# Making the first weight sum of a seven-product pair by two GpSimd transfers, and taking 43 pairs instead of 32 that way

## The chip, the cores and the metric

The kernel runs on one core of one Trainium2 chip. The metric is the device time of one execution in microseconds. The engines are named as the profile names them: PE is TensorE (PEld its weight loads), DVE is VectorE, ACT is ScalarE, POOL is GpSimd, and SP is SyncE, which here only issues transfers.

## The reference

An encoder trunk of two layers, width 2048, 256 tokens, 256 memory tokens, feed-forward width 8192, all in float32. Each layer has an attention sub-layer (12 heads, and 4 heads into the memory), an output projection, and a squared-ReLU feed-forward part. The change lies in that last part alone:

```python
for i in range(DEPTH):
    ...
    x = x + heads @ w_out[i]
    h = rms_norm(x, norm_mlp[i])
    x = x + jnp.square(jax.nn.relu(h @ w_up[i])) @ w_down[i]
```

`w_up[i]` is 2048 x 8192 and `w_down[i]` is 8192 x 2048.

## The kernel before, in words

Every float32 product is made of three matmuls: each operand is split into a high part (a rounded copy, by ACT) and a low part (the rest, by DVE), and PE adds high x high, high x low and low x high (`split` and `three`). PE works through the weights in pieces of 128 x 1024 (512 KB). SP loads a piece into `raw`, ACT casts it to `hi`, DVE subtracts to `lo`; each of the three has four buffers. `piece` hands a piece to PE and keeps two more in preparation (`AHEAD = 2`).

The down projection is done in two halves of 1024 output columns per layer (`half_`, or `h` in the plan). One half goes over 64 pieces, two at a time: pair `j` (0 to 31) covers 256 rows of the hidden and has two blocks of hidden rows, two blocks of tokens and two blocks of 512 columns, that is eight block products of three matmuls, 24 in all. The products of a half collect in four PSUM banks, `ps`.

For the pairs in `FAST` the eight block products are done as seven, by Strassen's scheme in Winograd's form (`seven`): 21 matmuls. They need sums of weight blocks and of hidden blocks, and four more PSUM banks, `side`, which `add_side` combines once after the last such pair. The sums of weights are made when the second piece of the pair is fetched (`fetch_sums`): `a` (two blocks side by side) is the first piece plus the upper half of the second piece, which is added to both; `b` is made from `a`, the first piece and the second piece, in two steps. `a` and `b` are then split like any other weights into `ah`, `al`, `bh`, `bl`.

These six tiles (128 x 1024 each) come from a pool of eight buffers called `x2`. In the second half of layer 0 four of the eight hold the next layer's input, so there `a` and `b` are taken from `blk`, ten buffers that hold the hidden and come free as it is used up. The middle part of the hidden lies in one large tile, `big`, which takes the relative-position bias of layer 1 as soon as it is free: SP copies it back, and POOL masks it with two selects (`bias_load`).

Engines work in order. The order is made when the program is built, by a scheduler that moves instructions among each other where their data allow; so the code's order is not the engines' order, and a look at it is given below.

Of the kernel before, what the change touches and what calls it, by code (L numbers as in the profile page):

```python
# [19 lines left out]
ALU = mybir.AluOpType  # L20
AX = mybir.AxisListType

P = 128
# [9 lines left out]
WAIT = 2  # L33
AHEAD = 2
WARM = 16
FAST = (5, 8, 11, 14, 17, 20, 23, 26)
LAM_INIT = 0.8 - 0.6 * math.exp(-0.3 * 0)

G_ATTN, G_MEM, G_MLP = 0, 2 * KT, 4 * KT
# [8 lines left out]
def trunk(ctx: ExitStack, tc: tile.TileContext, xin, xtok, memin, pos, rel, gcol, rows,  # L48
          w_a, w_b, w_mem, w_out, w_up, w_down, out):
    nc = tc.nc  # L50
# [10 lines left out]
    def nm(s):  # L61
        uid[0] += 1
        return f"{s}{uid[0]}"

    def bank(tag="aux"):
        return pp.tile([P, 512], F32, tag=tag, name=nm(tag))

    def quad(tag, shape=(P, 2, 2, 256), dt=F32R):
        return xp.tile(list(shape), dt, tag=tag, name=nm(tag), bufs={"x2": 8, "h2": 6, "blk": 10}[tag])
# [92 lines left out]
    def flush():  # L162
        while tasks:
# [3 lines left out]
    weights = {"a": w_a, "b": w_b, "mem0": w_mem[0], "mem1": w_mem[1], "out0": w_out[0], "out1": w_out[1],  # L167
               "up0": w_up[0], "up1": w_up[1], "down0": w_down[0], "down1": w_down[1]}
    plan = deque()

    def plan_chunks(name, chunks):
        plan.extend((name, c, j) for c in chunks for j in range(8))

    def plan_down(name):
        plan.extend((name, h, j) for h in range(2) for j in range(64))

# [12 lines left out]
    def fetch_sums(key, raw, hi, lo):  # L189

        first = newest[0]
        tag = "blk" if key[:2] == ("down0", 1) else "x2"
        a, b = quad(tag, (P, 2, 512), F32), quad(tag, (P, 2, 512), F32)
        nc.vector.tensor_tensor(a, first.rearrange("p (a n) -> p a n", a=2),
                                raw[:, 512:1024].unsqueeze(1).broadcast_to([P, 2, 512]), op=ALU.add)
        nc.vector.tensor_tensor(b[:, 0, :], a[:, 1, :], first[:, 0:512], op=ALU.add)
        nc.vector.tensor_tensor(b[:, 1, :], b[:, 0, :], raw[:, 0:512], op=ALU.add)
        split(hi[:, 0:512], lo[:, 0:512], raw[:, 0:512])
        ah, al, bh, bl = [quad("x2", (P, 2, 512)) for _ in range(4)]
        split(ah, al, a)  # L200
        split(bh, bl, b)
        sums[key] = (ah, al, bh, bl)

    def fetch(parts=1, lead=None):

        name, c, j = plan.popleft()
        src = weights[name][c, j]
        raw = wp.tile([P, 1024], F32, tag="raw", name=nm("raw"))
        hi = wp.tile([P, 1024], F32R, tag="hi", name=nm("hi"))
        lo = wp.tile([P, 1024], F32R, tag="lo", name=nm("lo"))  # L210
        n = 1024 // parts
        seven = name.startswith("down") and j % 2 == 1 and j // 2 in FAST
        for i in range(parts):
            s = slice(i * n, (i + 1) * n)
            if lead is not None:
                lead(i)
            behind[0] = nc.sync.dma_start(raw[:, s], src[:, s])
            if seven:
                fetch_sums((name, c, j), raw, hi, lo)
            else:  # L220
                split(hi[:, s], lo[:, s], raw[:, s])
        newest[0] = raw
        ready.append(((name, c, j), hi, lo))
# [16 lines left out]
    def split(hi, lo, src):  # L240
        nc.scalar.copy(hi, src)  # L241
        nc.vector.tensor_tensor(lo, src, as32(hi), op=ALU.subtract)  # L242
# [437 lines left out]
    def mlp(layer, X2, last):  # L680
# [24 lines left out]
        for half_ in range(2):  # L705
            tag = "mm" if half_ == 0 else "aux"
            ps = [[bank(tag) for _ in range(2)] for _ in range(2)]
            chunks = (2 * half_, 2 * half_ + 1)

            def three(bank_, first_, last_, x2, xs, w2, ws):  # L710
                nc.tensor.matmul(bank_, lhsT=x2[:, 0, xs], rhs=w2[0][:, ws], start=first_, stop=False)  # L711
                nc.tensor.matmul(bank_, lhsT=x2[:, 0, xs], rhs=w2[1][:, ws], start=False, stop=False)  # L712
                nc.tensor.matmul(bank_, lhsT=x2[:, 1, xs], rhs=w2[0][:, ws], start=False, stop=last_)  # L713

            lower, upper = slice(0, 512), slice(512, 1024)

            def mms(n, t, k, two, x2):
                w2 = two[(k + n) % 2]
                three(ps[n][t], k == 0, k == 4 * KT - 1, x2, slice((k % 2) * S + t * P, (k % 2) * S + (t + 1) * P), w2,
                      upper if n else lower)  # L720

            def seven(j, two, x2):

                ah, al, bh, bl = [v.rearrange("p a n -> p (a n)") for v in sums.pop((f"down{layer}", half_, 2 * j + 1))]
                t2 = quad("h2", (P, 2, 512))
                v = t2k([P, 512])
                h = hidden(j)
                h4 = h.rearrange("p (a s) -> p a s", a=4)
                nc.vector.tensor_tensor(v[:, 0:256].rearrange("p (a s) -> p a s", a=2), h4[:, 0:4:3, :],
                                        h4[:, 1:2, :].broadcast_to([P, 2, P]), op=ALU.subtract)  # L730
                nc.vector.tensor_tensor(v[:, 256:384], h[:, 384:512], v[:, 0:128], op=ALU.add)
                nc.vector.tensor_tensor(v[:, 384:512], h[:, 256:384], v[:, 256:384], op=ALU.subtract)
                split(t2[:, 0, :], t2[:, 1, :], v)
                at = [slice(i * P, (i + 1) * P) for i in range(4)]
                f, e = j == FAST[0], j == FAST[-1]
                three(side[0], f, e, x2, at[0], two[0], lower)
                three(ps[0][0], False, False, x2, at[2], two[1], lower)
                three(ps[1][0], False, False, t2, at[3], two[0], upper)
                three(side[1], f, e, t2, at[0], (ah, al), upper)
                three(side[3], f, e, t2, at[1], (ah, al), lower)  # L740
                three(side[2], f, e, t2, at[2], (bh, bl), lower)
                three(ps[0][1], False, False, x2, at[3], (bh, bl), upper)

            def add_to(n, t, src):
                c = chunks[n]
                d = xt[:, t, c * 512:(c + 1) * 512]
                nc.vector.scalar_tensor_tensor(d, src, r2[:, t:t + 1], d, op0=ALU.mult, op1=ALU.add)
                return c, d

            def add_side():  # L750

                q1, u2, u3, u4, u5 = [t2k([P, 512]) for _ in range(5)]
                nc.scalar.copy(q1, side[0])
                nc.vector.tensor_tensor(u2, side[2], q1, op=ALU.subtract)
                nc.vector.tensor_tensor(u4, side[1], u2, op=ALU.subtract)
                nc.vector.tensor_tensor(u3, u2, side[3], op=ALU.subtract)
                nc.vector.tensor_tensor(u5, u3, side[1], op=ALU.subtract)
                add_to(0, 0, q1)
                add_to(0, 1, u4)
                add_to(1, 0, u3)  # L760
                add_to(1, 1, u5)

            def finish(n, t):
                c, d = add_to(n, t, ps[n][t])
                if last:
                    nc.sync.dma_start(out[:, t * D + c * 512:t * D + (c + 1) * 512], d)

            held = []
            for j in range(32):
                if j == FAST[0]:  # L770
                    side = [bank("aux" if half_ == 0 else "mm") for _ in range(4)]
                two = [piece(f"down{layer}", half_, 2 * j + i) for i in range(2)]
                x2 = h2_of(j)
                if last and half_ == 1 and j >= 30:
                    held.append((j, two, x2))
                    continue
                if j in FAST:
                    seven(j, two, x2)
                else:
                    for kk in range(2):  # L780
                        for t in range(2):
                            for n in range(2):
                                mms(n, t, 2 * j + kk, two, x2)
                if j == FAST[-1]:
                    add_side()
                tick()
                tick()
            for n in range(2):
                for t in range(2):
                    for j, two, x2 in held:  # L790
                        for kk in range(2):
                            mms(n, t, 2 * j + kk, two, x2)
                    finish(n, t)
                if not last:
                    chunk_sq(chunks[n])
                    to_features(chunks[n], N2, G_ATTN + KT, tag)
# [73 lines left out]
    for g in range(3):  # L870
        ps = chunk_tok("b", g, X2)
        qT, qd = norm_T(ps, st1, 4, gs[:, 1:2])
        for h in range(4):
            n = 4 * g + h
# [71 lines left out]
```

## Time and profile before

| | |
|---|---|
| time, median of 3 runs | 2127.89 us (2127.4 to 2128.0) |
| the profiled execution | 2127.94 us, of which its span 2126.1 us |
| granted clock of TensorE | 0.999 |
| PE, DVE, ACT, POOL busy | 2116.4, 1497.5, 1130.8, 34.3 us |
| HBM read, mean rate | 401.93 MB, 192 GB/s |
| weight load of 512 KB for the down projection, from issue to landing | 4.3 us, median of 256 |

The down projection of layer 0 runs from about 785 to 1125 us of the span, that of layer 1 from about 1784 us to the end. PE is busy all the time, so the rows are to be read for two things: how many matmuls there are, and how far ahead of PE the other engines are when they deliver. A row of a group gives line, engine, operation, output and inputs, shapes and count, then busy time and mean duration, then the idle time before them and who ended it. A row of the timeline gives start, duration, and how many instructions were merged.

### The profile page before, as it was taken

The numbers are of one execution on the slowest core, as the hardware profiler recorded it, in microseconds if no ns is written. First come the engines' busy times: TensorE is split into PE (matmuls) and PEld (weight loads), VectorE is DVE, ScalarE is ACT, GpSimd is POOL, SyncE is SP. The second block draws the span as 40 slices with busy tenths as digits, with TensorE's granted clock in tenths as the row PEclk, the third lists the DMA queues.
The fourth block names the chain that finished last, engine by engine and source line by source line (L and its number), as shares of the span: only waits on it lengthen the run. The fifth ranks groups of instructions, "written<-read, shape, count | busy, mean of one in ns | idle before, by whom it ended". The sixth has DMA issues, their size and how long they took to land.

```text
span 2126.1 us, 29324 instructions
## 1 busy us (share of the span) xinstructions
PE 2116.4 (100%) x11020; PEld 1790.6 (84%) x11020; DVE 1497.5 (70%) x2259; ACT 1130.8 (53%) x1712; POOL 34.3 (2%) x61
## 2 busy tenths in 40 slices
PE   9999999999999999999999999999999999999999
PEld 7878878888888888888888888888888888888887
DVE  7667786566565558889886677655555556888896
ACT  6456675454444446656655566554444444665564
POOL 1200020000000000000000000000000000000000
PEclk9999999999999999999999999999999999999999
DMA  8864564666666655555766556466666666566654
GB/s 292 238 211 150 159 194 154 186 180 190 191 184 196 188 190 200 197 198 198 250 205 191 178 167 187 149 180 188 188 189 190 186 192 193 190 215 210 203 193 158
DMA packets 114958, 409.23 MB, mean 192 GB/s; under 512 B 13568, under 2 KB 14336, under 8 KB 114560
## 3 DMA queue, kind: packets, MB, share of 16 engines
q1 hardware_dynamic: 111840, 401.01, 59.7%
q0 software_dynamic: 1536, 4.20, 0.8%
q10 hardware_dynamic: 1440, 2.15, 0.3%
q8 instruction: 86, 1.41, 0.3%
q14 instruction: 56, 0.46, 0.1%
HBM read 401.93 MB, written 5.37 MB: 192 GB/s over the span
## 4 chain that ended last, share of the span: by engine, by line
PE 97%; DMA 1%; DVE 1%; ACT 1%; issue 0%; SPq 0%; POOL 0%; ACTq 0%; DVEq 0%; POOLq 0%
PE mm L325 11%; PE aux L325 11%; PE mm L312 9%; PE mm L314 9%; PE mm L313 9%; PE mm L329 6%; PE aux L329 6%; PE aux L711 5%; PE aux L712 5%; PE mm L711 5%; PE mm L712 5%; PE aux L713 5%; PE mm L713 5%; PE aux L404 1%; DMA raw<-in_w_a 1%; PE aux L375 1%
## 5 line engine op out<-in xcount | busy, mean ns | idle before, releaser
L242 DVE TENSOR_TENSOR lo<-raw,hi 128x1024 fp32r<-128x1024 f32 (+1 forms) x744 | 875.4, 1190 | 535.3 <-ACT hi L241 534.0
L241 ACT CAST hi<-raw 128x1024 fp32r<-128x1024 f32 (+1 forms) x744 | 751.7, 1024 | 760.9 <-PE aux L325 193.5
L312 PE MATMUL mm<-hi,x 128*128 128x512 f32 x704 | 281.5, 401 | 0.7 <-ACT hi L241 0.7
L313 PE MATMUL mm<-lo,x 128*128 128x512 f32 x704 | 276.8, 393 | 2.6 <-DVE lo L242 2.6
L314 PE MATMUL mm<-hi,x 128*128 128x512 f32 x704 | 276.5, 393 | 0.0
L325 PE MATMUL mm<-x,hi 128*128 128x512 f32 x1024 | 247.4, 391 | 0.0
L325 PE MATMUL aux<-x,hi 128*128 128x512 f32 x1024 | 246.9, 391 | 0.0
L325 PEld LDWEIGHTS mm<-x,hi 128*128 128x128 f32 x1024 | 188.2, 188 | 36.8 <-DVE xt L675 0.5
L325 PEld LDWEIGHTS aux<-x,hi 128*128 128x128 f32 x1024 | 188.2, 188 | 36.4
L712 PE MATMUL aux<-lo,h 128*128 128x512 f32 x432 | 168.2, 389 | 0.0
L713 PE MATMUL aux<-hi,h 128*128 128x512 f32 x432 | 168.1, 389 | 0.0
L711 PE MATMUL aux<-hi,h 128*128 128x512 f32 x432 | 168.1, 389 | 0.0
L711 PE MATMUL mm<-hi,h 128*128 128x512 f32 x432 | 168.0, 389 | 0.0
L712 PE MATMUL mm<-lo,h 128*128 128x512 f32 x432 | 168.0, 389 | 0.0
L713 PE MATMUL mm<-hi,h 128*128 128x512 f32 x432 | 168.0, 389 | 0.0
L313 PEld LDWEIGHTS mm<-lo,x 128*128 128x128 f32 x704 | 133.1, 189 | 28.4 <-DVE lo L242 4.2
L314 PEld LDWEIGHTS mm<-hi,x 128*128 128x128 f32 x704 | 132.6, 188 | 28.0
L312 PEld LDWEIGHTS mm<-hi,x 128*128 128x128 f32 x704 | 132.6, 189 | 27.2 <-ACT hi L241 1.3
L329 PEld LDWEIGHTS mm<-x,lo 128*128 128x128 f32 x1024 | 131.4, 191 | 4.8
L329 PEld LDWEIGHTS aux<-x,lo 128*128 128x128 f32 x1024 | 131.3, 191 | 5.0
L329 PE MATMUL mm<-x,lo 128*128 128x256 f32 x1024 | 133.3, 283 | 0.0
L329 PE MATMUL aux<-x,lo 128*128 128x256 f32 x1024 | 132.8, 283 | 0.0
(207 smaller groups left out, 2526.0 us busy)
## 6 DMA issues: line engine op xcount, KB each, us to landing
raw<-in_w_up SPq DMA_DIRECT2D x256, 512.0 KB, 3.8
raw<-in_w_down SPq DMA_DIRECT2D x256, 512.0 KB, 4.3
raw<-in_w_a SPq DMA_DIRECT2D x72, 512.0 KB, 4.0
raw<-in_w_out SPq DMA_DIRECT2D x64, 512.0 KB, 3.6
raw<-in_w_b SPq DMA_DIRECT2D x48, 512.0 KB, 3.7
raw<-in_w_mem SPq DMA_DIRECT2D x32, 512.0 KB, 4.0
raw<-in_w_a SPq DMA_DIRECT2D x16, 256.0 KB, 5.2
blk<-bkt POOLq DMA_DIRECT2D x32, 128.0 KB, 8.6
```

The source lines that it names most:

```text
L241: nc.scalar.copy(hi, src)
L242: nc.vector.tensor_tensor(lo, src, as32(hi), op=ALU.subtract)
L312: nc.tensor.matmul(ps[t], lhsT=xh, rhs=hi[:, ws], start=(k == 0), stop=False)
L313: nc.tensor.matmul(ps[t], lhsT=xh, rhs=lo[:, ws], start=False, stop=False)
L314: nc.tensor.matmul(ps[t], lhsT=xl, rhs=hi[:, ws], start=False, stop=(k == KT - 1))
L325: nc.tensor.matmul(ps[o], lhsT=hi[:, cols(k % 2, o)], rhs=x2.rearrange("p a s -> p (a s)"), start=(k == 0), stop=(k == 2 * nj - 1))
L329: nc.tensor.matmul(ps[o][:, 256:512], lhsT=lo[:, cols(k % 2, o)], rhs=x2[:, 0, :], start=False, stop=False)
L375: nc.tensor.transpose(out=pt[:, h * P:(h + 1) * P], in_=qn[t][:, h * P:(h + 1) * P], identity=ident)
L404: nc.tensor.transpose(out=pt[:, kt * S + qt * P:kt * S + (qt + 1) * P], in_=p_of(qt)[:, kt * P:(kt + 1) * P], identity=ident)
L711: nc.tensor.matmul(bank_, lhsT=x2[:, 0, xs], rhs=w2[0][:, ws], start=first_, stop=False)
L712: nc.tensor.matmul(bank_, lhsT=x2[:, 0, xs], rhs=w2[1][:, ws], start=False, stop=False)
L713: nc.tensor.matmul(bank_, lhsT=x2[:, 1, xs], rhs=w2[0][:, ws], start=False, stop=last_)
```

## The change

Three things. `a` is no longer added by DVE from `raw`: POOL's queue loads the first piece a second time from HBM straight into `a`, and then issues a second transfer that reads the upper half of the second piece, twice, and adds it to what lies in `a`. The list of pairs is denser: 11 pairs in the halves that use `FAST`, two in every five, instead of 8, one in three. And the second half of layer 0 has a list of its own, `LATE`, with 10 pairs. Together that is 3 x 11 + 10 = 43 pairs instead of 4 x 8 = 32.

```diff
-FAST = (5, 8, 11, 14, 17, 20, 23, 26)
+FAST = (3, 5, 8, 10, 13, 15, 18, 20, 23, 25, 28)
+LATE = (6, 8, 11, 13, 16, 18, 21, 23, 26, 28)
...
+    def fast_pairs(name, h):
+        return LATE if (name, h) == ("down0", 1) else FAST
...
         a, b = quad(tag, (P, 2, 512), F32), quad(tag, (P, 2, 512), F32)
-        nc.vector.tensor_tensor(a, first.rearrange("p (a n) -> p a n", a=2),
-                                raw[:, 512:1024].unsqueeze(1).broadcast_to([P, 2, 512]), op=ALU.add)
+        src = weights[key[0]][key[1]]
+        nc.gpsimd.dma_start(a, src[key[2] - 1].rearrange("p (a n) -> p a n", a=2))
+        nc.gpsimd.dma_start(a, src[key[2]][:, 512:1024].unsqueeze(1).broadcast_to([P, 2, 512]), accum_op=ALU.add)
         nc.vector.tensor_tensor(b[:, 0, :], a[:, 1, :], first[:, 0:512], op=ALU.add)
         nc.vector.tensor_tensor(b[:, 1, :], b[:, 0, :], raw[:, 0:512], op=ALU.add)
...
-        seven = name.startswith("down") and j % 2 == 1 and j // 2 in FAST
+        seven = name.startswith("down") and j % 2 == 1 and j // 2 in fast_pairs(name, c)
...
+            fast = fast_pairs(f"down{layer}", half_)
...
-                f, e = j == FAST[0], j == FAST[-1]
+                f, e = j == fast[0], j == fast[-1]
...
-                if j in FAST:
+                if j in fast:
                     seven(j, two, x2)
...
-                if j == FAST[-1]:
+                if j == fast[-1]:
                     add_side()
```

The change adds six lines ahead of most of the code. So after it the two transfers are L199 and L200, the two steps of `b` are L201 and L202 (L196 and L197 before; the sum of `a` was L194), the split is L246 and L247 (L241 and L242), and the selects are L621 and L623 (L616 and L618).

How DVE is ordered around pair 23 in the first half of layer 0, before: `x21674` is `a`, `x21675` is `b`, `x21677` and `x21679` are the low parts of the two, `raw1668` and `raw1671` the two pieces of the pair, `h...` splits of the hidden for other pairs.

```order
L242 TENSOR_TENSOR h21709_8902<-blk1354_7167,h21709_8902 128x512
L194 TENSOR_TENSOR x21674_8753<-raw1668_8743,raw1671_8749 128x1024
L196 TENSOR_TENSOR x21675_8754<-x21674_8753,raw1668_8743 128x512
L197 TENSOR_TENSOR x21675_8754<-x21675_8754,raw1671_8749 128x512
L242 TENSOR_TENSOR x21677_8761<-x21674_8753,x21676_8760 128x1024
L242 TENSOR_TENSOR x21679_8763<-x21675_8754,x21678_8762 128x1024
L242 TENSOR_TENSOR lo1670_8745<-raw1668_8743,hi1669_8744 128x1024
L242 TENSOR_TENSOR lo1673_8751<-raw1671_8749,hi1672_8750 128x512
```

The same place after: `x21690` is `a` (now written by the transfers), `x21691` is `b`, `x21693` and `x21695` are their low parts, `raw1684` and `raw1687` the two pieces, and the first two rows are the pieces of pair 22.

```order
L247 TENSOR_TENSOR lo1679_8748<-raw1677_8746,hi1678_8747 128x1024
L247 TENSOR_TENSOR lo1682_8754<-raw1680_8752,hi1681_8753 128x1024
L201 TENSOR_TENSOR x21691_8796<-x21690_8795,raw1684_8785 128x512
L247 TENSOR_TENSOR h21718_8907<-blk1354_7167,h21718_8907 128x512
L202 TENSOR_TENSOR x21691_8796<-x21691_8796,raw1687_8791 128x512
L247 TENSOR_TENSOR x21693_8804<-x21690_8795,x21692_8803 128x1024
L247 TENSOR_TENSOR h21725_8946<-blk1354_7167,h21725_8946 128x512
L247 TENSOR_TENSOR x21695_8806<-x21691_8796,x21694_8805 128x1024
L247 TENSOR_TENSOR lo1686_8787<-raw1684_8785,hi1685_8786 128x1024
```

The row of the first sum is gone, and two splits of the hidden now stand between the steps; the first row that needs the transfers is L201, and `lo1686`, which PE needs first in the pair, stands behind it.

On POOL, which before had nothing between the norm of the memory and the two selects, the transfers of the second half of layer 0 stand before and behind the selects. After (`blk1997` is `a` of pair 21, `blk2019` of pair 23, `blk2048` of pair 26):

```order
L199 DMA blk1997_10201<-in_w_down 128x1024
L200 DMA blk1997_10201<-in_w_down 128x2x512
L621 AFFINE_SELECT big2116_10758<-big2116_10758 128x12x128
L623 AFFINE_SELECT big2116_10758<-big2116_10758 128x12x128
L199 DMA blk2019_10297<-in_w_down 128x1024
L200 DMA blk2019_10297<-in_w_down 128x2x512
L199 DMA blk2048_10432<-in_w_down 128x1024
```

Before, in the same place:

```order
L254 TENSOR_TENSOR acc_100<-acc_100,t1k692_3459 128x256
L254 TENSOR_TENSOR acc_100<-acc_100,t1k693_3462 128x256
L616 AFFINE_SELECT big2076_10652<-big2076_10652 128x12x128
L618 AFFINE_SELECT big2076_10652<-big2076_10652 128x12x128
L941 UNCONDITIONAL_BRANCH
```

The transfers of pair 23 and of all later pairs of this half have moved behind the selects, which themselves wait for SP's copy into `big`.

More of the change, by code (lines that the diff above doesn't have):

```diff
@@ L769, in mlp @@
             for j in range(32):
-                if j == FAST[0]:
+                if j == fast[0]:
                     side = [bank("aux" if half_ == 0 else "mm") for _ in range(4)]
```

## The prediction

> **What bounds the kernel now.** I read the page first, then the busy time by stretch, then single rows of TensorE and VectorE inside a seven-product pair.
>
> ```profile
> span 2126.1 us, 29324 instructions
> PE   2116.4 (100%) x11020; PEld 1790.6 (84%) x11020; DVE 1497.5 (70%) x2259; ACT 1130.8 (53%) x1712; POOL 34.3 (2%) x61
> PE 97%; DMA 1%; DVE 1%; ACT 1%; issue 0%; SPq 0%; POOL 0%; ACTq 0%; DVEq 0%; POOLq 0%
> L712 PE MATMUL aux<-lo,h 128*128 128x512 f32 x432 | 168.2, 389 | 0.0
> L712 PE MATMUL mm<-lo,h 128*128 128x512 f32 x432 | 168.0, 389 | 0.0
> ```
>
> PE (TensorE) carries 97% of the chain that ended last, and the matmuls of the down projection never stand behind an idle PE (0.0 in the last column). So a matmul that is left out there is worth its full pitch, and anything that makes PE wait there is paid in full. The pitch is read from the starts, since the 389 ns of one matmul overlap the next. These are the first and the last row of seven-product pair 11 in the first half of layer 0, and the first row of pair 12:
>
> ```profile
> 843.81 0.39 PE L711 MATMUL aux<-hi,h 128*128 128x512 f32 x1
> 844.04 0.39 PE L712 MATMUL aux<-lo,h 128*128 128x512 f32 x1
> ...
> 848.35 0.39 PE L713 MATMUL mm<-x,h 128*128 128x512 f32 x1
> 848.57 0.39 PE L711 MATMUL mm<-hi,h 128*128 128x512 f32 x1
> ```
>
> 21 matmuls take 848.57 - 843.81 = 4.76 us, 0.2267 us each; an ordinary pair has 24 and takes 5.44 us. What runs beside it is seen in two stretches (PE, PEld, DVE, ACT, POOL busy, granted clock, share of the DMA engines, GB/s):
>
> ```profile
> 811.00:961.00 150.00, 150.00 (x668) 124.32 (x667) 130.16 (x153) 91.71 (x118) 0.00 (x0) 1.00 0.59 202
> 1811.00:1961.00 150.00, 150.00 (x663) 124.21 (x662) 132.21 (x164) 89.69 (x110) 0.00 (x0) 1.00 0.62 209
> ```
>
> DVE (VectorE) is 87% busy there, ACT 61%, POOL (GpSimd) not at all, and the clock is whole. DVE is the next engine in line.
>
> **What the change takes off PE.** 11 pairs more go by seven products: 11 x 3 = 33 matmuls fewer, 33 x 0.2267 = 7.48 us. The profiled execution took 2127.94 us (its span is 2126.1; the median of the runs is 2127.89), so with no new wait it would take 2120.5 us. Nothing in the change can bring more than that, since PE has no idle time in these stages to give back.
>
> **What it does to DVE and ACT.**
>
> ```profile
> L242 DVE TENSOR_TENSOR x<-x,x 128x1024 fp32r<-128x1024 f32 x48 | 58.3, 1221 | 0.0
> L242 DVE TENSOR_TENSOR lo<-raw,hi 128x512 fp32r<-128x512 f32 x48 | 32.9, 686 | 0.2
> L194 DVE TENSOR_TENSOR x<-raw,raw 128x1024 f32<-128x1024 f32 x24 | 29.4, 1224 | 11.4 <-DMA raw<-in_w_down 11.4
> L242 DVE TENSOR_TENSOR h<-t2k,h 128x512 fp32r<-128x512 f32 x32 | 21.9, 684 | 0.0
> L197 DVE TENSOR_TENSOR x<-x,raw 128x512 f32<-128x512 f32 x24 | 16.6, 691 | 0.7
> L241 ACT CAST x<-x 128x1024 fp32r<-128x1024 f32 x48 | 50.6, 1053 | 82.1 <-DVE x L194 74.9 <-DVE x L197 7.2
> ```
>
> The first sum leaves DVE: 32 x 1.22 = 39 us less. Each further seven costs DVE two sums of 0.69, two low parts of 1.22, one low part of 0.68, three small differences (0.42 for the first, its row stands in the next group; the two others are half its size, so about 1.0 together is an estimate), and saves 0.54 on the half piece: about 5.0 us, 11 times, 55 us. So DVE does 16 us more over four halves, 4 us each. In 150 us it stands idle for 20, so I cost this at nothing; if that cover were gone, the 4 us a half would show as waits of PE for `lo`. ACT gains two casts of 1.05 for each further seven, beside 39% idle: nothing.
>
> **What it puts on the path: two transfers in a row.** `a` is now loaded by POOL's queue, POOL waits for the landing, then issues the accumulating transfer, and DVE's L201 waits for that. Behind L201 on DVE, which works in order, stand the splits that PE needs next. So the question is how long the two take (call it D) and how long they may take.
>
> How long they may: a seven uses six of the eight x2 buffers, so where FAST holds in the x2 pool the load of `a` can start only when PE is through with the seven before the last. For pair 23 that is pair 18. From the end of 18 to the start of 23 PE has pairs 19, 21, 22 (24 matmuls each) and seven 20 (21): 93 x 0.2267 = 21.1 us. Of this DVE needs a last part for itself:
>
> ```profile
> 833.98 1.28 DVE L242 TENSOR_TENSOR h<-big,h 128x512 fp32r<-128x512 f32 x2
> 836.56 1.23 DVE L194 TENSOR_TENSOR x<-raw,raw 128x1024 f32<-128x1024 f32 x1 [1.30 <-DMA raw<-in_w_down]
> 837.82 0.69 DVE L196 TENSOR_TENSOR x<-x,raw 128x512 f32<-128x512 f32 x1
> 838.55 0.69 DVE L197 TENSOR_TENSOR x<-x,raw 128x512 f32<-128x512 f32 x1
> 839.16 2.42 DVE L242 TENSOR_TENSOR x<-x,x 128x1024 fp32r<-128x1024 f32 x2
> 841.50 1.82 DVE L242 TENSOR_TENSOR lo<-raw,hi 128x1024 fp32r<-128x1024 f32 x2
> 821.14 0.42 DVE L729 TENSOR_TENSOR t2k<-blk 128x256 f32<-128x256 f32 x1
> ```
>
> From the start of `b` to the end of the first piece's `lo` the trace shows 841.50 + 1.22 - 837.82 = 4.9 us; in the new order two `h` splits (1.28) stand in between as well: 6.2 us. So D may be 21.1 - 6.2 = 14.9 us before PE waits. That holds at pairs 8, 13, 18, 23 and 28 of the three halves that use FAST, 15 places; pairs 10, 15, 20 and 25 have their first `lo` ahead of the rest and bear some 4 us more. In the LATE half `a` and `b` have buffers of their own kind, which DVE frees early.
>
> How long they take: the trace has no accumulating transfer and no load of 512 KB by POOL. The nearest rows:
>
> ```profile
> raw<-in_w_down SPq DMA_DIRECT2D x256, 512.0 KB, 4.3
> blk<-bkt POOLq DMA_DIRECT2D x32, 128.0 KB, 8.6
> big<-bsv SPq DMA_DIRECT2D x1, 3072.0 KB, 12.2
> DMA to landing us min/median/max: 3.8/8.6/9.5
> L593 POOL DMA_DIRECT2D blk<-bkt x32: 489/489/744, 49.6 to 79.3; - x32
> ```
>
> The fourth row is that of L593, whose 32 transfers were queued behind each other. The first ones, alone, landed after 3.8 us with 128 KB. 384 KB more at the stage's 202 GB/s are 1.95 us: 5.75 us for the load. The accumulating one must also read what it adds to, 512 KB, 1.8 us at the 292 GB/s of the page's fastest slice:
>
> ```profile
> GB/s 292 238 211 150 159 194 154 186 180 190 191 184 196 188 190 200 197 198 198 250 205 191 178 167 187 149 180 188 188 189 190 186 192 193 190 215 210 203 193 158
> ```
>
> That makes 7.55, and D = 13.3 us, an estimate 1.6 us under the limit. The bounds: below, two loads as SP has them, 2 x 4.3 = 8.6; above, two as POOL's queue had them when full, 2 x 9.5 = 19. I take 13.3 since POOL's queue will hold one transfer at a time, like the first of L593, but beside raw loads.
>
> The Trainium skill, "DMA: Bandwidth & Descriptors", section "Anatomy of one DMA — SWDGE (gpsimd) path", gives 2.0 us plus the bytes over 436 GB/s for a transfer of this path: 3.2 us for 512 KB, D near 6.4 as an estimate, with no wait anywhere and 2120.5 us. The 3.8 us measured for 128 KB are against it (the formula gives 2.3), so I do not use it.
>
> **One place with a longer chain.** In the second half of layer 0 the bias for layer 1 comes back into the tile that held part of the hidden, and POOL's two selects on it now stand ahead of the transfers of pair 23.
>
> ```profile
> 1049.97 1.55 POOL L616 TENSOR_SCALAR_AFFINE_SELECT big<-big 128x1536 f32<-128x1536 f32 x1 [744.21 <-DMA big<-bsv]
> 1051.47 2.00 POOL L618 TENSOR_SCALAR_AFFINE_SELECT big<-big 128x1536 f32<-128x1536 f32 x1
> ```
>
> The chain is the copy (12.2 us), the selects (3.5) and D (13.3): 29.0 us. It starts when DVE has split the last `h` of that tile, pair 19's. In the new order this stands right behind the first split of seven 18's sums, by my count of the rows 7.4 us before pair 19 begins. From there to pair 23 PE has 93 matmuls, 21.1 us, and the first split of pair 23's sums is due 2.3 us later, after 3.5 us of DVE's work: 7.4 + 21.1 + 2.3 - 3.5 = 27.3. So PE waits some 1.5 to 2 us once; I take 1.5, between none (D under 11.6) and 7.4 (D = 19). In the run before nothing waited for these selects.
>
> **The sum.** 2127.94 - 7.48 + 1.5 = 2122.0 us.
>
> **The rivals.** *The two transfers outlast their cover* (slower). From D = 14.9 each us more costs 15 us over the 15 places, plus 1 us at the selects; at 15.15 the 7.5 us are spent, 15 x 0.25 = 3.7 of them here and 12.2 + 3.5 + 15.15 - 27.3 = 3.6 at the selects. At D = 16.3 it is 15 x 1.4 = 21, and 12.2 + 3.5 + 16.3 - 27.3 = 4.7: 2127.94 - 7.48 + 21 + 4.7 = 2146. For it: POOL's full queue landed 128 KB only every 1.05 us or so (8.6 us with eight in flight), and raw loads share the engines. Against it: DMA engines stand 41% idle in the stage. Chance 0.33.
>
> *Raw loads come late* (slower). 43 x 1 MB is written on top of what the four halves load, and the adding reads a third time: per half some 11 MB to 17 MB in 170 us, 65 to 100 GB/s over 202.
>
> ```profile
> L194 DVE TENSOR_TENSOR blk<-raw,raw x8: 1211/1226/1227, 973.5 to 1084.4; 128x1024 f32<-128x1024 f32 x8
> DMA to landing us min/median/max: 3.3/4.3/8.0
> ```
>
> The second row is that of the weight loads between 785 and 1114 us; the 8.0 fell beside the 3 MB copy and made no wait of PE. If half of the 43 pairs saw loads 3.7 us late (8.0 - 4.3), the first `lo` of a seven, done 1.3 us ahead (842.72 against 844.04) and 1.2 us earlier now that the sum is gone, would come 1.2 us late: 21 x 1.2 = 25, 2146 us. Chance 0.08. The same page of the Trainium skill, section "Issuing engines are not separate DMA queues", says that all issuers' transfers run on the same 16 engines and interleave, which speaks for this rival; the stretch at the copy agrees, at 8.0 us.
>
> *The gain is given back almost whole* (no change): D between 14.7 and 15.4, some 2124 to 2132 us. Chance 0.12.
>
> **How the numbers follow.** A measurement of this kernel can tell about 0.2%, 4.3 us, from no change. The forecast, with D under 14.7, has 0.47, all of it under 2123.6. So faster 0.47, same 0.12, slower 0.33 + 0.08 = 0.41. The likeliest case alone spans 2120 to 2123.6. The range starts at 2120.5 less 0.7 for the spread of runs (2127.4 to 2128.0), 2119.8, and reaches to D = 16.5, 2150, which leaves out under 2 in 10. Signs are mixed, so the likeliest case decides the point.
>
> **What would show it.** Right: the down projection's matmuls 33 fewer, 0.23 us pitch, no PE idle before them except a few us in the second half of layer 0; the landing of L199 near 5.8 and of L200 near 7.5 us; DVE idle at L201 without PE idle. Wrong: PE waiting for DVE `lo` or `x` at pairs 8, 13, 18, 23, 28, with L201 waiting for the transfer; L199 and L200 together over 14.9 us; or DVE waiting for `raw`.

## The result, and the profile after

The changed kernel takes 2142.23 us (median of 4 runs, 2141.24 to 2147.18) beside 2127.94 us for the kernel before on the same chip: 0.71% slower, ratio 1.0071 with an interval of 1.0054 to 1.0089. Forecast were 2122.0 us and a gain; the time lies inside the stated range, but on the side of the rivals.

From the page of the changed kernel (span, busy times, shares of the chain that ended last, two groups of matmuls):

```profile
span 2139.8 us, 29550 instructions
PE 2115.5 (99%) x10987; PEld 1783.6 (83%) x10987; DVE 1502.8 (70%) x2315; ACT 1150.1 (54%) x1745; POOL 111.3 (5%) x147
PE 79%; DMA 10%; DVE 6%; issue 4%; ACT 1%; POOL 0%; SPq 0%; DVEq 0%; POOLq 0%; ACTq 0%
L718 PE MATMUL aux<-lo,h 128*128 128x512 f32 x408 | 160.1, 392 | 7.2 <-DVE lo L247 7.2
L718 PE MATMUL mm<-lo,h 128*128 128x512 f32 x401 | 156.9, 391 | 5.4 <-DVE lo L247 5.4
```

The 33 matmuls are gone (11020 to 10987). In exchange PE now waits for `lo` in the down projection, where it waited for nothing, and PE's share of the chain falls from 97% to 79%, with DMA at 10%. Taking all starts of matmuls there, and counting what each step exceeds 0.2267 us, the changed kernel loses 21.4 us more than the kernel before. 21.4 less the 7.5 saved is 13.9; the span grew by 13.7.

By stretch (PE, PEld, DVE, ACT, POOL busy, granted clock, share of the DMA engines, GB/s), the same two stretches as in the prediction:

```profile
811.00:961.00 150.00, 145.57 (x631) 119.12 (x630) 124.17 (x151) 91.51 (x118) 17.12 (x19) 0.99 0.81 256
1811.00:1961.00 150.00, 148.55 (x654) 122.40 (x653) 128.99 (x159) 93.95 (x118) 19.46 (x22) 1.00 0.88 276
```

DVE is no busier than before (124 and 129 us against 130 and 132). What has changed is the DMA engines: 0.81 and 0.88 of them are busy, against 0.59 and 0.62. Those are means. Cut into 40 slices (each digit is the busy share of one slice in tenths), the stretch from 811 to 961 us has 3 slices of 90% and more before (first row) and 19 after (second row):

```profile
DMA  7580857329933886189607770778058828457446
DMA  5993999798688995893799879939999880887299
```

The page's queues (packets, MB, share of 16 engines over the whole span) and its transfers (median us to landing) say what that does:

```profile
q1 hardware_dynamic: 111840, 401.01, 57.4%
q0 software_dynamic: 19424, 49.29, 10.1%
raw<-in_w_down SPq DMA_DIRECT2D x256, 512.0 KB, 5.1
x<-in_w_down POOLq DMA_DIRECT2D x66, 512.0 KB, 5.8
```

The weight loads of the down projection land after 5.1 us in the median instead of 4.3. Those issued between 785 and 955 us, before and after:

```profile
DMA to landing us min/median/max: 3.3/4.3/5.8
DMA to landing us min/median/max: 3.5/5.2/8.9
```

Of the 62 after, 17 take over 6 us. Among the second pieces of the seven-product pairs, which DVE needs for `b`, 13 of 43 take over 7 us; before, none of 32 did. The two transfers of a pair, from POOL's issue of the first to the landing of the second, take 13.27 us in the mean, between 9.9 and 18.1. In 40 of the 43 pairs the sum had landed before the pair's second raw piece, by 3.8 us in the median over all 43. Both kinds of lateness reach DVE. What DVE waited for at the two steps of `b` (us, times), first L201, then L202, and last, for comparison, what it waited for before at its own first sum, L194:

```profile
  DMA raw<-in_w_down: 38.9, 24
  DMA x<-in_w_down: 18.7, 5
  DMA blk<-in_w_down: 1.5, 1
...
  DMA raw<-in_w_down: 17.1, 10
...
  DMA raw<-in_w_down: 15.2, 22
```

Raw loads cost DVE 56.0 us at its two steps, the transfers 20.2, against 15.2 us for raw before. Two places show how this arrives at PE. Pair 13 in the first half of layer 0 is held up by a raw load (timeline, DVE's rows and then PE's):

```profile
845.55 0.69 DVE L201 TENSOR_TENSOR x<-x,raw 128x512 f32<-128x512 f32 x1
846.15 0.69 DVE L247 TENSOR_TENSOR h<-big,h 128x512 fp32r<-128x512 f32 x1
850.50 0.69 DVE L202 TENSOR_TENSOR x<-x,raw 128x512 f32<-128x512 f32 x1 [3.66 <-DMA raw<-in_w_down]
854.32 1.82 DVE L247 TENSOR_TENSOR lo<-raw,hi 128x1024 fp32r<-128x1024 f32 x2
...
853.28 0.50 PE L717 MATMUL aux<-hi,h 128*128 128x512 f32 x1
855.59 0.51 PE L718 MATMUL aux<-lo,h 128*128 128x512 f32 x1 [1.81 <-DVE lo L247]
```

L201 has its sum in time. L202 stands 3.66 us for the second piece of the pair, and PE gets `lo` 2.08 us late (855.59 - 853.28 - 0.23). Pair 18 is held up by the transfers:

```profile
860.53 0.58 POOL L199 DMA_DIRECT2D x<-in_w_down  x1 [8.83 <-PE mm L719]
868.48 1.20 POOL L200 DMA_DIRECT2D x<-in_w_down  x1 [7.38 <-DVE lo L247]
...
878.64 0.69 DVE L201 TENSOR_TENSOR x<-x,raw 128x512 f32<-128x512 f32 x1 [6.02 <-DMA x<-in_w_down]
...
882.61 0.49 PE L717 MATMUL aux<-hi,h 128*128 128x512 f32 x1 [1.07 <-ACT hi L246]
884.60 0.50 PE L718 MATMUL aux<-lo,h 128*128 128x512 f32 x1 [1.49 <-DVE lo L247]
886.47 0.63 PE L718 MATMUL mm<-lo,h 128*128 128x512 f32 x1
```

POOL waits for PE as foretold, then the first transfer takes 7.66 us and the second 10.13: 18.1 us. (The second row names DVE as what POOL waited for; the first transfer landed at 868.19 us, just before it.) While the second one was under way POOL issued the first transfer of pair 20, at 870.73 us, and that took 10.36 us.

Going through all waits of PE of 0.3 us and more and the rows of DVE and ACT ahead of each: 12.3 us, at eight places, follow a raw load, 4.3 us follow the transfers, 0.5 us neither. Of the 12.3, 9.6 us follow loads that took 7.0 to 7.8 us; 2.7 us follow loads that took 3.6 and 4.6 us but were issued late, since DVE, itself held up by an earlier late load, gave their buffer back late. The rest of the 21.4 is 1.6 us of slower matmuls behind pair 18 (below) and small steps. By half the loss is 7.3, 5.4, 2.1 and 6.7 us.

### The profile page after: what moved, and what is told of

Read it like the earlier page. It is cut to its first block, busy times and chain, and to the rows that moved or that the text cites. A ratio compares the mean times of both kernels' runs of the same rounds, so it can differ in the third digit from the quotient of the medians.

```text
span 2139.8 us, 29550 instructions
## 1 busy us (share of the span) xinstructions
PE 2115.5 (99%) x10987; PEld 1783.6 (83%) x10987; DVE 1502.8 (70%) x2315; ACT 1150.1 (54%) x1745; POOL 111.3 (5%) x147
## 3 DMA queue, kind: packets, MB, share of 16 engines
q0 software_dynamic: 19424, 49.29, 10.1%
## 4 chain that ended last, share of the span: by engine, by line
PE 79%; DMA 10%; DVE 6%; issue 4%; ACT 1%; POOL 0%; SPq 0%; DVEq 0%; POOLq 0%; ACTq 0%
PE mm L330 11%; PE aux L330 11%; PE mm L317 8%; PE mm L319 8%; PE mm L318 8%; PE mm L334 6%; PE aux L334 6%; DMA raw<-in_w_down 4%; PE mm L718 3%; PE mm L719 3%; PE mm L717 3%; PE aux L718 3%; PE aux L719 2%; PE aux L717 2%; DVE lo L247 2%
## 5 line engine op out<-in xcount | busy, mean ns | idle before, releaser
L247 DVE TENSOR_TENSOR lo<-raw,hi 128x1024 fp32r<-128x1024 f32 (+1 forms) x744 | 870.8, 1182 | 479.6 <-ACT hi L246 478.4
L246 ACT CAST hi<-raw 128x1024 fp32r<-128x1024 f32 (+1 forms) x744 | 748.0, 1017 | 755.0 <-PE aux L330 196.1
L330 PEld LDWEIGHTS aux<-x,hi 128*128 128x128 f32 x1024 | 188.3, 188 | 36.3
L718 PE MATMUL aux<-lo,h 128*128 128x512 f32 x408 | 160.1, 392 | 7.2 <-DVE lo L247 7.2
L718 PE MATMUL mm<-lo,h 128*128 128x512 f32 x401 | 156.9, 391 | 5.4 <-DVE lo L247 5.4
L717 PE MATMUL aux<-hi,h 128*128 128x512 f32 x408 | 159.1, 390 | 1.1 <-ACT hi L246 1.1
L719 PE MATMUL aux<-hi,h 128*128 128x512 f32 x408 | 159.0, 390 | 0.0
L717 PE MATMUL mm<-hi,h 128*128 128x512 f32 x401 | 156.7, 391 | 0.3 <-ACT hi L246 0.3
L719 PE MATMUL mm<-hi,h 128*128 128x512 f32 x401 | 156.6, 391 | 0.0
```

Source lines behind the costliest of these rows:

```text
L330: nc.tensor.matmul(ps[o], lhsT=hi[:, cols(k % 2, o)], rhs=x2.rearrange("p a s -> p (a s)"), start=(k == 0), stop=(k == 2 * nj - 1))
```

## The experiments

Theory A: the two transfers take DMA engines from the raw loads and from each other, and what lands late makes DVE and then PE wait. Theory B: the chain of two transfers is too long for its cover, whatever else runs. Theory C: 43 pairs are too many for DVE. "Lost" is PE's loss in the down projection over that of the kernel before, worked out as above from the one profiled execution of each run; "raw" is the median landing of its 256 loads, in us as all times. The runs of the kernel before spread from 2125.5 to 2130.2, which is about what a single run can be off.

| run | us | lost | raw | chain of transfers, mean |
|---|---|---|---|---|
| before | 2127.9 | 0 | 4.3 | none |
| the change | 2142.2 | 21.4 | 5.1 | 13.3 |
| dve_sum | 2125.7 | 6.4 | 4.3 | none |
| traffic | 2155.3 (one run) | 36.3 | 5.3 | nobody waits |
| chain3 | 2118.6 (one run) | 0.2 | 4.5 | 12.3 |
| chain4 | 2131.4 (one run) | 12.0 | 4.5 | 15.3 |
| chain5 | 2186.2 (one run) | 68.0 | 4.5 | 19.0 |
| first_only | 2124.0 (one run) | 2.5 | 4.5 | one transfer |
| plain2 | 2127.4 (one run) | 8.8 | 5.0 | 11.6 |
| old_list | 2131.0 | 2.6 | 5.0 | 13.8 |
| raw5 | 2187.6 | 58.6 | 5.4 | 15.2 |
| pool_sum | 2186.0 | 65.7 | 4.3 | none |
| dve_mixed | 2121.0 | 0.0 | 4.3 | none |

**dve_sum.** The change's lists without its transfers.

```diff
-        nc.gpsimd.dma_start(a, ...)
-        nc.gpsimd.dma_start(a, ..., accum_op=ALU.add)
+        nc.vector.tensor_tensor(a, first..., raw[:, 512:1024]..., op=ALU.add)
```

> The lists of the changed kernel (43 pairs by seven products), but the first weight sum is made by DVE from raw, as before; no extra transfers. Theory A (the two transfers take DMA bandwidth from the raw loads and from each other, and everything lands late) and theory B (the two transfers one after the other are too long for the time between two uses of a buffer, whatever else runs) both expect the full gain: 2120.5 to 2123 us, PE without waits in the down projection, raw landing at a median of 4.3 us. Theory C (43 pairs ask too much of DVE or of the buffers, with or without the transfers) expects PE to wait for lo: 2128 us or more.

2125.69 us (11 runs, 2123.13 to 2128.42), ratio 0.9990 (0.9981 to 0.9999), between what A and B and what C expected. In the profiled execution (2128.4 us, the longest of them) 0.4 us of the loss fall in layer 1, 0.2 in the first half of layer 0, and 5.8 us between 1050 and 1090 us, in the second half of layer 0, where the 3 MB copy runs and a raw load took 10.5 us. So 43 pairs are not too many for DVE in the three halves that use FAST; C holds, if at all, in the other one. There the changed kernel lost 5.4 us, no more than this run, so these runs don't show that its loss in that half is the transfers' doing.

**traffic.** The transfers beside DVE's sum, with nobody waiting for them (the diff is against dve_sum; the sources, as in the change, are left out).

```diff
+        sc = dp.tile([P, 2, 512], F32, tag="sc", name=nm("sc"), bufs=2)
+        tiny = small(1)
+        nc.scalar.copy(tiny, newest[0][:, 0:1])
+        nc.gpsimd.dma_start(sc[:, 0, 0:1], tiny)
+        nc.gpsimd.dma_start(sc, ...)
+        nc.gpsimd.dma_start(sc, ..., accum_op=ALU.add)
```

> As the run with DVE's sum, and beside it the two transfers of each of the 43 pairs are issued all the same, but into a scratch tile in HBM that nobody reads, begun by a small copy of ACT at the time of the pair's raw loads; nobody waits for them. Theory A expects raw landings at a median near 5.2 us as in the changed kernel, and more than half of its 21 us of waits: 2130 to 2142 us. Theory B expects no waits of PE: 2120.5 to 2124 us.

2155.3 us, more than either theory expected: PE loses 36.3 us, 29.9 more than without the transfers, though no instruction of DVE or PE depends on them. Its DMA engines stand at 0.86 busy in both of the stretches above; between 785 and 955 us raw lands after

```profile
DMA to landing us min/median/max: 3.5/5.8/8.9
```

against 4.3 in the median of dve_sum there. B can't make this, since no chain is waited for; nor does any of PE's waits of 0.3 us and more lead back to ACT's small copy. So A is shown in kind: transfers that nobody waits for make raw late and cost PE time. Its size is not that of the change. DVE here carries the sum as well, the transfers write to HBM, and a third, small one begins each pair; what each of these adds was not tried.

**chain5, chain4, chain3.** A chain of POOL transfers with next to no bytes, to price the length alone (the sum is missing; `src` as in the change).

```diff
-        nc.gpsimd.dma_start(a, ...)
-        nc.gpsimd.dma_start(a, ..., accum_op=ALU.add)
+        nc.gpsimd.memset(a, 0.0)
+        for k in range(5):        # 4, 3
+            nc.gpsimd.dma_start(a[:, 0, 0:64], src[key[2] - 1][:, k * 64:k * 64 + 64])
```

> The changed kernel with its two transfers replaced by a memset of POOL and five transfers of 32 KB each, one after the other into the same place (the sum is not made), so the same wait of DVE on a chain of POOL transfers, estimated at 12 to 16 us, with 0.16 MB a pair in place of 1 MB. Theory B expects the waits of the changed kernel, 2130 to 2145 us. Theory A expects raw landings at 4.3 us and waits only where the chain is over 14.9 us: 2120.5 to 2124 us.

> As the chain of five, with four transfers of 32 KB: by the chain of five (18.8 us in the mean, 0.97 of it the memset, 3.6 for each transfer) it takes 15.2 us, longer than the 13.3 us of the changed kernel's two transfers, with raw landing near 4.5 us. Theory A expects less loss than in the changed kernel: under 15 us of PE's time in the down projection, 2122 to 2135 us. Theory B expects more than there: over 23 us, 2143 us or more.

> The same with three transfers, 11.6 us, below the 14.9 us of the prediction's cover and below the 13.3 us of the changed kernel. Theory A expects next to no waits, 2120.5 to 2124 us. Theory B in its strict form (the cover is well under 13 us) expects waits of 5 us or more in all: 2126 to 2135 us.

A transfer of 32 KB takes nearly as long as one of 128 KB alone (3.8 us); this is the row of the chain of five:

```profile
DMA to landing us min/median/max: 1.9/3.4/6.1
```

So the chain of five takes 19.0 us in the mean, not 12 to 16, and is no test at the length of the change. Chain4 came out as A expected, with 12.0 us lost, and chain3 too, but the three runs show less about the length than was meant. Their transfers write into the first half of `a`, and the first step of `b` reads the second half: in none of the three did DVE wait for a transfer at the steps of `b`. What waited was ACT's cast of `a`, which comes later; in chain4 (L247, us, times):

```profile
  DMA x<-in_w_down: 86.0, 16
```

A chain therefore has longer there than in the change, and chain4's 12.0 us beside the change's 21.4 don't decide between A and B. In chain5 POOL itself is the limit: it had stood idle for over 0.3 us before only 8 of its 43 chains, against 40 in chain3 and 23 in chain4. What stays is that POOL's chains as such need not cost anything. Chain3, 12.3 us long, gives the whole gain, with raw at 4.5 us and DVE 88% busy:

```profile
811.00:961.00 150.00, 150.00 (x667) 124.35 (x666) 131.33 (x169) 95.37 (x127) 26.00 (x41) 1.00 0.62 208
```

**first_only and plain2.** Which of the two transfers loads the engines (both leave part of the sum out).

```diff
 first_only:
-        nc.gpsimd.dma_start(a, src[key[2]][:, 512:1024]..., accum_op=ALU.add)
 plain2:
-        nc.gpsimd.dma_start(a, src[key[2]][:, 512:1024]..., accum_op=ALU.add)
+        nc.gpsimd.dma_start(a, src[key[2]][:, 512:1024]...)
```

> The changed kernel without the accumulating transfer (a is only the first piece, so the sum is missing): half the added bytes, and a chain of one transfer of 5 to 6 us. Theory A expects a part of the waits, raw landings at a median of 4.5 to 4.8 us: 2121 to 2128 us. Theory B expects none: 2120.5 to 2121.5 us.

> The changed kernel, but the second transfer writes instead of adding (a is the upper half twice, so the sum is missing): the same source, the same pieces of 2 KB, the same chain. If the adding is what loads the DMA engines (the transfers of POOL's queue hold 10.1% of the engines in the changed kernel and 3.8% with the first transfer alone), their share falls to 7% or less, the second transfer to 5.5 us or less in the median, and most of the waits go: 2121 to 2130 us. If the pieces of 2 KB do it, all stays: 2138 to 2145 us.

POOL's queue on the page (packets, MB, share of 16 engines), of first_only and of plain2:

```profile
q0 software_dynamic: 7728, 26.74, 3.8%
```

```profile
q0 software_dynamic: 13920, 49.29, 6.9%
```

The second transfer moves the same 22.55 MB whether it adds or not. Writing, it takes 6.9 - 3.8 = 3.1% of the engines; adding, 10.1 - 3.8 = 6.3%, twice as much. Without the adding it lands after 5.0 us in the mean instead of 6.6, the chain takes 11.6, and the loss falls from 21.4 to 8.8 us. With the first transfer alone only 2.5 us are left, as A expected; the chain is shorter there too, so this run can't tell the two apart. The median landing of raw in plain2 is still 5.0 us, and 18 of 64 between 785 and 955 us take over 6 us, as in the change. But of the second pieces of its pairs only 6 of 43 take over 7 us, against 13, and the waits of PE behind raw loads fall from 12.3 to 4.8 us, those behind the transfers from 4.3 to 2.7.

**old_list.** The transfers with the pairs of the kernel before.

```diff
-FAST = (3, 5, 8, 10, 13, 15, 18, 20, 23, 25, 28)
-LATE = (6, 8, 11, 13, 16, 18, 21, 23, 26, 28)
+FAST = (5, 8, 11, 14, 17, 20, 23, 26)
+LATE = FAST
```

> Only one part of the change: the two transfers make the first sum, but for the 32 pairs of the kernel before. The next use of a buffer is one ordinary pair further away: by the prediction's working the cover is 26.5 - 6.2 = 20.3 us, which the two transfers never exceeded in the changed kernel (9.9 to 18.1). If only the length of the chain counts, no waits: 2127 to 2128 us. If raw loads that land late beside the transfers count by themselves, raw landings at a median near 4.8 us, and some 5 us of waits: 2130 to 2135 us.

2130.96 us (10 runs), ratio 1.0016 (1.0007 to 1.0025). DVE never waited for a transfer there, only for raw, which landed after 5.0 us; PE's loss in the profiled execution, 2.6 us, lies around 1057 us in the second half of layer 0, where raw loads take up to 9.6 us. So even sparsely used the transfers cost a little and bring nothing, since DVE had the time for the sum. In the three other halves PE lost nothing here, 0.6 us in dve_sum, and 16 us in the change: there neither the transfers nor the dense list costs much alone, and the two together do.

**raw5.** One more buffer for the raw pieces.

```diff
-        raw = wp.tile([P, 1024], F32, tag="raw", name=nm("raw"))
+        raw = wp.tile([P, 1024], F32, tag="raw", name=nm("raw"), bufs=5)
...
-        return tp.tile([P, 256], F32, tag="t1k", name=nm("t1k"), bufs=4)
+        return tp.tile([P, 256], F32, tag="t1k", name=nm("t1k"), bufs=2)
...
-        return tp.tile([P, n], F32, tag="sm", name=nm("sm"), bufs=36)
+        return tp.tile([P, n], F32, tag="sm", name=nm("sm"), bufs=25)
```

> The changed kernel with five buffers for the raw pieces in place of four, so that SP can issue each raw load one piece (some 2.7 us) earlier; the room is taken from two pools of small tiles (t1k 2 for 4, sm 25 for 36). Theory A (what makes PE wait is mostly raw loads that land late) expects most of the 23 us that PE loses in the down projection to go, 10 us or less left, and the wait of DVE for raw with it: 2122 to 2133 us. Theory B (the chain of the two transfers is too long for its cover) expects the waits to stay: 2140 us.

2187.64 us, ratio 1.0286 (1.0247 to 1.0325): neither expectation held. With a raw load more in flight the transfers are what lands late. The first transfer of a pair, L199:

```profile
DMA to landing us min/median/max: 4.3/7.0/13.5
```

(5.9 in the median of the changed kernel), the chain takes 15.2 us in the mean and up to 22.7, and of the 33 chains in the halves with FAST 19 exceed the 14.9 us of the cover, instead of 6. DVE at L201, by what it waited for:

```profile
  DMA x<-in_w_down: 75.3, 15
  DMA raw<-in_w_down: 23.1, 8
```

The transfers' part rises from 18.7 to 75.3 us as raw's falls from 38.9 to 23.1. That fits raw loads and transfers taking from one another, seen from the other side. What part the smaller pools of small tiles have in the loss was not tried.

**pool_sum.** The first sum by an addition of POOL.

```diff
-        nc.vector.tensor_tensor(a, first..., raw[:, 512:1024]..., op=ALU.add)
+        nc.gpsimd.tensor_tensor(a, first..., raw[:, 512:1024]..., op=ALU.add)
```

(The diff is against dve_sum.)

> The lists of the changed kernel, and the first sum is made by an addition of POOL from raw: no extra transfers, and nothing added to DVE, which is 95% busy in the run with DVE's sum (142.4 of 150 us). POOL's additions of 128x256 took 0.74 us, so 128x1024 is estimated at 3 us. If that is hidden, the gain of 7.5 us less a microsecond or two: 2120.5 to 2123 us. If DVE is slowed beside POOL (the splits of h took up to 3.54 us for two beside POOL's selects, 2.4 when alone) or raw buffers come free late: 2124 to 2130 us.

2185.99 us, ratio 1.0270 (1.0256 to 1.0284), far beyond what I expected. (The 2.4 us of the expectation are two splits of 128x1024; two of `h`, 128x512, take 1.28 us when alone.) The addition takes 2.4 us, twice DVE's 1.22, and can't begin before the second raw piece is there. Its row, and what DVE waited for at the first step of `b`:

```profile
L198 POOL TENSOR_TENSOR x<-raw,raw x33: 2383/2397/3783, 794.1 to 2151.9; 128x1024 f32<-128x1024 f32 x33
...
  POOL x L198: 83.0, 27
  POOL blk L198: 23.1, 7
```

POOL waited for the raw piece 30 times of 43, and the sum is then as late as the raw load plus 2.4 us. The transfers' one merit is that they need no raw piece: in the changed kernel the first one starts 18 us, in the median, before the pair's second raw piece lands.

**dve_mixed.** The candidate: dve_sum, with the old list in the second half of layer 0 (the diff is against dve_sum).

```diff
-LATE = (6, 8, 11, 13, 16, 18, 21, 23, 26, 28)
+LATE = (5, 8, 11, 14, 17, 20, 23, 26)
```

> A candidate for a better kernel: DVE makes the first sum, 11 pairs in the three halves that use FAST, and the 8 pairs of the kernel before in the second half of layer 0 (41 pairs in all). In the run with 43 pairs and DVE's sum, 5.8 of the 6.5 us that PE lost against before fell in that half, between 1050 and 1080 us. 27 matmuls fewer than before are 6.1 us: 2121 to 2123 us if nothing else waits, 2125 us or more if DVE at 95% busy is what costs.

2121.03 us (7 runs, 2119.78 to 2122.69), ratio 0.9970 (0.9959 to 0.9981): 0.3% faster than the kernel before, with no loss of PE. DVE is 95% busy (142.60 of 150) and the DMA engines as before:

```profile
811.00:961.00 150.00, 150.00 (x668) 124.28 (x667) 142.60 (x175) 97.23 (x127) 0.00 (x0) 1.00 0.60 202
```

## Why the prediction was wrong, point by point

- *33 matmuls at 0.2267 us.* Right: 7.48 us, as chain3 shows, where the starts of matmuls give the whole of it back.
- *DVE and ACT at nothing.* Right, and more than it said: with the sum left on DVE there is still no wait of PE in dve_mixed, whose three halves with FAST have the pairs of the change. There the sum did not have to leave.
- *The cover, 14.9 us.* Right, by the changed kernel's own rows. Among the 15 places three chains made PE wait: pair 18 (18.08 us long, 2.99 lost), pair 8 in the first half of layer 1 (15.13, 0.52) and pair 28 in its second half (15.86, 0.77). Length less loss is 15.1, 14.6 and 15.1. No shorter chain there made PE wait, and chains of 16.3 to 16.8 us at pairs 10, 20 and 25 did not either, as the text said of these pairs.
- *How long the two transfers take, 13.3 us.* Right as a mean, 13.27, in part by luck: 6.3 and 6.6, with a gap of 0.34, where the text had 5.75 and 7.55, so two errors cancel. Its reason, that POOL's queue holds one transfer at a time, does not hold: in 19 of the 43 pairs the next pair's first transfer was issued before the second had landed, and those second ones took 7.1 us in the mean, the others 6.3. And one number for all pairs was too little: the chains run from 9.9 to 18.1 us, and those over the cover cost 4.3 us and 1.6 us of slow matmuls, while the mean is under it. The forecast held that a D under 14.7 had no wait.
- *Raw loads come late.* This is the step that failed. The sum had no term for it, and the rival had 0.08, against 12.3 of the 21.4 us lost. Its own working named the price (21 places by 1.2 us, 25 us), near the 1.5 us, in the mean, at each of eight places. Its condition, half of the pairs with loads 3.7 us late, was too hard: 13 of the 43 second pieces took over 7 us, and that was enough. At six of the places a single wait of DVE of 1.9 to 3.7 us came through to PE as 1.3 to 2.1 us, so the slack was some 0.6 to 1.8 us. The text's one argument on load, the 41% of the DMA engines that stood idle (given against the other rival), is a mean over 150 us: 3 of 40 slices were full before, and 19 with the transfers. And the second transfer was counted as another 512 KB read; it held the engines twice as long as a plain one (6.3% against 3.1%).
- The Trainium skill, "DMA: Bandwidth & Descriptors", section "Rules for kernel authors", says that an accumulating transfer reads its destination and writes it later; the doubled share fits. The same page of the Trainium skill, section "Issuing engines are not separate DMA queues", which the prediction set beside the rival of 0.08, points at what cost most: raw landed after 5.1 us against 4.3.
- *The selects, 1.5 us once.* Too high: the transfers of pair 23 in that half took 10.2 us, so that copy, selects and transfers together took 25.2 us, less than the 27.3 that the text allowed. PE lost about 0.3 us there, at 1073 us.
- *The rivals.* The first (chains that outlast their cover) was real and accounts for 5.9 of the 21.4 us with the slow matmuls; the second for 12.3. Only together do they give the time. The second needs the dense list as well: with the old list raw landed after 5.0 us too, and PE lost 2.6 us.

## What to carry to other kernels

A transfer moved off an engine is not free because the DMA engines show idle time in the mean: ask how much later every other transfer of that stage lands, and how much slack those have. The accumulating transfer here counted twice, by its share of the engines. And work should be moved off an engine only if the stage shows that the engine is late, and not merely that its busy share is high: in dve_mixed DVE at 95% busy carried the sum without a wait of PE.

## What the runs showed that was not expected

- Two waits of PE close together can slow the matmuls behind them. Behind pair 18, where PE ran one matmul between 881.4 and 884.6 us, eight matmuls follow each other at some 0.42 us instead of 0.227 (the row at 886.47 has 0.63 us in place of 0.39), and the granted clock between 886 and 892 us is 0.75. The Trainium skill, "TensorE: Matmul & The Clock Gate", section "What's actually happening", has the clock halved after an idle window of about 3.4 us. The row agrees in the rate and not in the idling: PE stood still for 1.07 and 1.49 us, with one matmul in between. In raw5 the same pace follows at eight places, for five to eight matmuls.
- The issue of the accumulating transfer holds POOL for 1.20 us; the same transfer without the adding 0.71.
- A transfer of 32 KB from POOL's queue takes 3.3 to 3.6 us in the median of the three chain runs, so a chain of such small ones is set by its count.
